# An encoder layer on one core: copies of a branch's tokens six tiles ahead, that branch's outputs kept in DRAM as 2 KB rows, and some low parts on VectorE alone

## The chip, the core and the metric

The kernel runs on one core of a Trainium2 chip. The metric is device time in microseconds (us) of one execution; three executions of the kernel before took 1133.49, 1138.85 and 1132.47, median 1133.49. A profiled execution took 1135.29 us, of which its trace covers a span of 1133.5.

The core's engines run side by side and each takes its own instructions strictly in order. In the profile PE is TensorE's matmuls and PEld its weight loads, DVE is VectorE, ACT is ScalarE, POOL is GpSimd and SP is SyncE, which here issues every DMA.

## The reference

One encoder layer is applied with the same weights to two token batches, a prompt of 512 tokens and a sample of 1024, both 1024 wide, all in fp32:

```python
h = rmsnorm(x, norm_g)
qa, ka, va, za, qb, kb, vb, zb, ga, gb = split(h @ w_in)      # 1024 -> 5376
oa = neighbourhood_attention(norm(qa), norm(ka), va, rpb_a) * silu(za)   # branch A: 8 heads of 64, 2-D window
ob = window_gqa_attention(norm(qb), norm(kb), vb, t5, sink) * silu(zb)   # branch B: 8 query heads, 2 key heads, band of 128
merged = sigmoid(ga) * (oa @ w_o_a) + sigmoid(gb) * (ob @ w_o_b)
y = x + merged @ w_out
```

## The kernel before

**Split operands.** fp32 accuracy on TensorE comes from splitting each operand into a high part (rounded by ScalarE to the matmul's type) and a low part (what is left, a subtraction), and adding three products: high by high, high by low and low by high. So `whi`/`wlo` are the parts of a weight tile, `hh`/`hl` those of the normalized tokens h, `T` holds both parts of sums of h, `pp` those of attention weights. The high part is always a ScalarE copy. The low part is a subtraction in `split` (line 1177), which may go to VectorE or to GpSimd, whichever the planner finds free first.

**Stages.** The prompt is normalized and goes through its attention; then its dense phase runs (gates z, merge gates g, the two output projections, `w_out`), during which the sample's h is made; then the sample's attention and its dense phase. The token axis is cut into tiles of 128: 4 for the prompt, 8 for the sample.

**Attention.** Six groups run one after the other, four pairs of heads of branch A (A0 to A3) and two of branch B (B0, B1). Within a group, `project` (line 764) multiplies one token tile by 384 columns of weights in 24 matmuls of 384 columns. ScalarE squares the result (`sq`, 783), VectorE sums (`ss`, 788), GpSimd turns the sum into a reciprocal root (`rs_v` 795, `rs_r` 802), VectorE scales (`qk`, 819) and TensorE transposes q and k (`x<-ident,qk`, 864). `attend` then makes scores, exponentials and outputs; the output goes from the accumulator to a tile `ot_` (1073) and from there by SP to DRAM. Since TensorE works on the projection of later tiles meanwhile, the chain from `sq` to `qk` runs beside it. Filler matmuls (`d<-hh,fh`, parts of the merge gates) are put into the gaps.

Branch B takes its tokens in another order: token tile t is every nb-th column of h (nb tiles). Those columns are first copied together into four tiles `hb` of 512 columns (two halves of `hh`, two of `hl`; lines 665 on ScalarE, 667 on VectorE). There are four `hb` buffers, one token tile's worth. The copies wait only for all of h and for a free buffer, and their priority is that of the tile before the one they serve.

**Branch outputs.** `o_d` in DRAM holds, for each channel chunk c (c below 4 is branch A, 4 to 7 branch B), 128 channels by all tokens. Branch B's outputs exist as two halves e whose sum is the output. They are stored tile by tile, in two DMAs per tile, in B's token order (line 1102). The z step of the dense phase loads them (line 1535): a block of 512 tokens in natural order is `512/nb` tokens of each of the nb tiles, so a load of the sample's half takes 8 runs of 64 values (256 B) for each channel, one of the prompt's 4 runs of 128 values (512 B). The two loaded halves are added (`ot<-ot`), multiplied with silu(z) and stored as `u_d`.

**Sums.** Most of the sample's dense phase runs a scheme with seven instead of eight products per block of four, which needs sums of h and of weights. The sums of h were stored in `t_d` during the prompt's dense phase; `stored_sums` (1245) loads them in 16 pieces of 512 columns (four sums j, four chunks k each) and splits each into parts `T`. `pair_strassen` makes weight sums `S` from raw tiles (1166) and `weight_tiles` splits them. The products `x<-T`, `d<-T` and `p<-T` (lines 1293 to 1295) need all parts.

**What sets the order.** Every operation is recorded with a priority, a duration for each engine that may take it and what it depends on. `Flow.run` then walks through a model of time and gives each engine, whenever the model says that it is free, its ready operation of best priority; the order in which it hands them out is the order of the instructions. Where VectorE and GpSimd could both take an operation, the operation carries the mark `port`; while one with that mark runs on one of the two engines in the model, no marked one is begun on the other. An operation that only VectorE may take has no such mark unless it is given one. The real order of waiting is the one on the chip; the model's times do not appear there.

Of the kernel before, what the change touches and what calls it, by code (L numbers as in the profile page):

```python
# [10 lines left out]
F32 = mybir.dt.float32  # L11
# [15 lines left out]
SLACK = 1.1  # L27
SCRATCH = 1024
# [12 lines left out]
P = 128  # L41
# [313 lines left out]
def encoder_kernel(  # L355
# [23 lines left out]
    nc = tc.nc  # L379
# [24 lines left out]
    o_d = {geo.nt: dpool.tile([2, 8, P, geo.nt], F32, tag=f"o_d{geo.nt}", name=f"o_d{geo.nt}") for geo in (gp, gs)}  # L404
# [246 lines left out]
    def attention_phase(geo, hh, hl, h_ops, mask_d, early, late):  # L651
# [79 lines left out]
        def project(br, w, t, prio):  # L731
# [10 lines left out]
            else:  # L742
# [6 lines left out]
                for q in range(2):  # L749
                    for m, v in enumerate((hh, hl)):  # L750
# [5 lines left out]
                            prio - 1, new=[hb[m][q]], hold=[v], after=[o for u in h_ops.values() for o in u], port=True,  # L756
# [204 lines left out]
        def weigh(br, gi, g, block, sums, pss, sbs, nb_t, info, prio):  # L961
# [114 lines left out]
            if br == "A":  # L1076
# [10 lines left out]
                def emit():  # L1087
                    if len(runs) == 1:
                        dst = over(o_d[nt][0, g], runs).rearrange("(i p) n -> p i n", i=2)
                        nc.sync.dma_start(dst, ot.t[:64, ::2])  # L1090
                        return
                    for i in range(2):
                        dst = over(o_d[nt][0, g, 64 * i : 64 * i + 64], runs)
# [3 lines left out]
            else:  # L1097
                for e in range(2):
                    dst = o_d[nt][e, 4 + 2 * g : 6 + 2 * g, :, runs[0][0] : runs[0][0] + P]
                    dst = dst.rearrange("c (i d) n -> d (c i) n", d=64)  # L1100
                    o = sp(
                        lambda e=e, dst=dst: nc.sync.dma_start(dst, ot.t[e * 64 : e * 64 + 64]),
                        131072, prio, use=[ot],
                    )
                    for c in (4 + 2 * g, 5 + 2 * g):
                        for n in range(nt // 512):
                            stores[c, n].append(o)
# [31 lines left out]
    def dense_phase(geo, hh, hl, h_ops, o_stores, exps_done, start, opened, tp, up, p0, p1, p2, x_t, y_t, classic, fill, after_gates=None, side=None):  # L1139
# [28 lines left out]
        def split(hi, lo, src, n, prio, new_hi, new_lo, src_v, after=()):  # L1168
# [7 lines left out]
                any_tt(n),  # L1176
# [59 lines left out]
        def stored_sums(prio, d, after):  # L1236

            tv, ops = {}, {}
            for j in (1, 2, 0, 3):
                tv[j] = tuple(f.value(tp, [P, 4, nh], F32R, "T", 8) for _ in range(2))  # L1240
                vh, vl = tv[j]
                for k in range(4):
# [7 lines left out]
                        (vh, k == 0), (vl, k == 0), [st],  # L1250
# [9 lines left out]
        def weight_tiles(operands, per, prio):  # L1260
# [5 lines left out]
            for i, src in enumerate(operands):  # L1266
                at, q = [], 0
                while q < 4:
# [7 lines left out]
                        (hi, ti not in seen), (lo, ti not in seen), [src],  # L1276
# [72 lines left out]
        def pair_strassen(srcs, post, prio, mov_h, mov_t, seed=None, last=False, kept=None):  # L1349
# [11 lines left out]
            w = weight_tiles([*first, s2, s3, s1, raw[1, 1], s4], 6, prio - 0.5)  # L1361
# [162 lines left out]
        def post_z(c, a, n, v, in_psum, prio):  # L1524
# [3 lines left out]
            for e, ot in enumerate(ots):  # L1528
                if c < 4:
                    src, dst = o_d[nt][e, c, :, a : a + n], lambda ot=ot: ot.t[:, :n]  # L1530
# [423 lines left out]
```

## Time and profile before

| | before |
|---|---|
| executions, us | 1133.49, 1138.85, 1132.47 (median 1133.49) |
| profiled execution | 1135.29 us, span of its trace 1133.5 us |
| PE | 1119.0 us busy, 6079 instructions |
| PEld | 973.2 us |
| DVE | 860.1 us, 1988 instructions |
| ACT | 651.9 us, 1499 |
| POOL | 337.3 us, 438 |
| DMA | 184.91 MB in 139010 packets on SP's queue; 167 GB/s of HBM traffic over the span |

The stages can be told apart by their matmuls: the last product of the prompt's attention (line 1066) starts 216 us from the start of the trace, its dense phase goes on to about 394, the sample's attention runs from there to about 786, and the sample's dense phase to the end. A row of the timeline gives the start of an instruction, how long it took, its engine, the line, the operation, what it writes and reads, and in brackets how long the engine had been idle before it and what ended that. An `xN` row is N like instructions in a row. The matmuls of a row overlap: one of 512 columns is shown with 0.39 us, and the next begins 0.23 us after it.

### The profile page before, as it was taken

How to read it: one execution, taken by the hardware profiler on the slowest of the kernel's cores; microseconds unless marked ns; L12 is line 12 of the kernel's file. 1: busy time of each engine (PE TensorE's matmuls, PEld its weight loads, DVE VectorE, ACT ScalarE, POOL GpSimd, SP SyncE). 2: the span in 40 equal slices, each digit the busy share in tenths (PEclk: the TensorE clock that was granted, in tenths of full speed). 3: DMA queues.
4: the chain of work that ended last, by engine and by line, in shares of the span. 5: the costliest groups of instructions: out<-in, count | busy, mean ns of one | idle time of the engine just before them, and what ended most of it. 6: DMA issues, size and time to landing. Idle time of an engine off the chain costs nothing.

```text
span 1133.5 us, 18690 instructions
## 1 busy us (share of the span) xinstructions
PE 1119.0 (99%) x6079; PEld 973.2 (86%) x6079; DVE 860.1 (76%) x1988; ACT 651.9 (58%) x1499; POOL 337.3 (30%) x438
## 2 busy tenths in 40 slices
PE   8999999999999999999999999999999999999998
PEld 6999988888888889999999988988788888888887
DVE  5888797587776568787878888885988766677764
ACT  6777987644432257565769888876543335423430
POOL 4653433000011154434324344420333322222211
PEclk9999999999999999999999999999999999999999
DMA  7854543488886732121212314244977645867862
GB/s 263 276 155 138 184 115 103 110 257 248 256 278 216 254 128 91 27 63 30 82 41 85 81 38 112 57 131 121 307 241 234 224 156 170 281 207 222 280 215 93
DMA packets 139108, 186.11 MB, mean 164 GB/s; under 512 B 29897, under 2 KB 68561, under 8 KB 139010
## 3 DMA queue, kind: packets, MB, share of 16 engines
q1 hardware_dynamic: 139010, 184.91, 51.8%
q8 instruction: 48, 0.79, 0.3%
q14 instruction: 50, 0.41, 0.1%
HBM read 137.66 MB, written 51.92 MB: 167 GB/s over the span
## 4 chain that ended last, share of the span: by engine, by line
PE 93%; DMA 2%; DVE 2%; issue 1%; ACT 1%; POOL 1%; SPq 0%; DVEq 0%; ACTq 0%
PE p L764 25%; PE x L1294 9%; PE x L1295 9%; PE x L1293 9%; PE x L1066 5%; PE x L937 5%; PE x L1029 5%; PE d L1293 4%; PE d L1295 4%; PE d L1294 4%; PE p L1294 4%; PE p L1295 4%; PE p L1293 4%; PE x L864 2%; DMA w<-in_w_att_dram 1%
## 5 line engine op out<-in xcount | busy, mean ns | idle before, releaser
L764 PE MATMUL p<-whi,hh 128*128 128x384 f32 x384 | 133.4, 348 | 0.0
L764 PE MATMUL p<-whi,hl 128*128 128x384 f32 x384 | 132.2, 344 | 0.0
L764 PE MATMUL p<-wlo,hh 128*128 128x384 f32 x384 | 131.8, 343 | 0.0
L1172 ACT ACTIVATE whi<-raw 128x512 fp32r<-128x512 f32 (+1 forms) x140 | 81.4, 600 | 71.2 <-PE x L1294 22.3
L981 ACT ACTIVATE sb<-sb,mx 128x384 f32<-128x384 f32 (+1 forms) x192 | 107.8, 565 | 16.9 <-DVE mx L972 16.5
L1295 PE MATMUL x<-T,wlo 128*128 128x512 f32 x280 | 108.9, 389 | 0.0
L1294 PE MATMUL x<-T,whi 128*128 128x512 f32 x280 | 108.9, 389 | 0.0
L1293 PE MATMUL x<-T,whi 128*128 128x512 f32 x280 | 108.9, 389 | 0.0
L764 PE MATMUL p<-whi,hb 128*128 128x384 f32 x384 | 107.6, 346 | 0.0
L1177 POOL TENSOR_TENSOR wlo<-raw,whi 128x512 fp32r<-128x512 f32 (+1 forms) x33 | 39.5, 1204 | 215.6 <-DMA raw<-in_w_g_dram 112.9
L1040 DVE TENSOR_TENSOR pp<-x,pp 128x512 fp32r<-128x512 f32 (+1 forms) x136 | 82.5, 638 | 19.6 <-ACT pp L1035 19.0
L1177 DVE TENSOR_TENSOR wlo<-raw,whi 128x512 fp32r<-128x512 f32 (+1 forms) x107 | 72.0, 682 | 32.3 <-ACT whi L1172 28.7
L802 POOL TENSOR_TENSOR rs_r<-rs_v,mhalf 128x4 f32<-128x4 f32 (+1 forms) x72 | 80.5, 1118 | 5.7
L1035 ACT ACTIVATE pp<-x 128x512 fp32r<-128x512 f32 (+1 forms) x136 | 70.8, 559 | 15.8 <-PE x L1029 14.3
L1294 PE MATMUL x<-hl,whi 128*128 128x512 f32 x200 | 77.8, 389 | 0.0
L1295 PE MATMUL x<-hh,wlo 128*128 128x512 f32 x200 | 77.8, 389 | 0.0
L1293 PE MATMUL x<-hh,whi 128*128 128x512 f32 x200 | 77.8, 389 | 0.0
L1066 PE MATMUL x<-pp,v 128*128 128x256 f32 (+1 forms) x368 | 75.8, 322 | 0.0
L764 PEld LDWEIGHTS p<-whi,hl 128*128 128x128 f32 x384 | 72.6, 189 | 1.3 <-issue 1.0
L764 PEld LDWEIGHTS p<-wlo,hh 128*128 128x128 f32 x384 | 72.7, 189 | 1.0 <-issue 0.7
L764 PEld LDWEIGHTS p<-whi,hh 128*128 128x128 f32 x384 | 72.7, 189 | 0.7 <-DVE v L812 0.3
L764 PEld LDWEIGHTS p<-whi,hb 128*128 128x128 f32 x384 | 69.1, 188 | 3.1 <-issue 1.3
(388 smaller groups left out, 2965.1 us busy)
## 6 DMA issues: line engine op xcount, KB each, us to landing
raw<-in_w_g_dram SPq DMA_DIRECT2D x84, 256.0 KB
w<-in_w_att_dram SPq DMA_DIRECT2D x46, 384.0 KB
raw<-in_w_z_dram SPq DMA_DIRECT2D x40, 256.0 KB
ot<-o_d SPq DMA_DIRECT2D x36, 256.0 KB
g_d<-C SPq DMA_DIRECT2D x34, 256.0 KB
fr<-in_w_g_dram SPq DMA_DIRECT2D x28, 256.0 KB
raw<-in_w_out_dram SPq DMA_DIRECT2D x28, 256.0 KB
out_dram<-C SPq DMA_DIRECT2D x19, 256.0 KB
```

What stands on the lines that cost most here:

```text
L764: pe.matmul(ps.t[:, :GW], part[u](k), mv.t[:, c], start=k == 0 and m == 0, stop=k == KC - 1 and m == 2,)
L802: lambda e: nc.gpsimd.tensor_tensor(r.t[:, :nn], rv.t[:, :nn], mhalf[:, :nn], op=ALU.pow),
L937: pe.matmul(pss[2 * pair + i].t[:, :width], q.t[rows, u, at : at + P], kv[:, tiles[0] : tiles[-1] + 1 : step], start=n == 0, stop=n == 2,)
L981: act.activation(sb.t[:, :width], sb.t[:, :width], AF.Exp, bias=mx.t[:, i : i + 1], scale=-1.0, accum_out=sm.t[:, i : i + 1],)
L1035: lambda e, pt=pt, pp=pp, nn=nn: act.activation(pp.t[:, 0, :nn], pt.t[:, :nn], AF.Copy),
L1040: lambda e, pt=pt, pp=pp, nn=nn: dve.tensor_tensor(pp.t[:, 1, :nn], pt.t[:, :nn], pp.t[:, 0, :nn].bitcast(F32), op=ALU.subtract),
L1066: pe.matmul(out(), v.t[:, vs], mv(), start=first, stop=last)
L1172: (("act", ACT_(n)),), lambda e: act.activation(hi(), src(), AF.Copy), prio,
L1177: lambda e: engines[e].tensor_tensor(lo(), src(), hi().bitcast(F32), op=ALU.subtract), prio,
L1293: pe.matmul(out, hi.t[:, cs], mh(), start=first and k == 0, stop=False, **more)
L1294: pe.matmul(out, hi.t[:, cs], ml(), start=False, stop=False, **more)
L1295: pe.matmul(out, lo.t[:, cs], mh(), start=False, stop=last and k == len(ws) - 1, **more)
```

## The change

1. **Copies of branch B's tokens.** The `hb` copies of a tile now also wait for the first matmul of the projection that stands six tiles (`AHEAD`) ahead of the tile before it, so those of a stage's first B tile are no longer ready as soon as h is. For later tiles the buffers decide as before.
2. **Branch B's outputs in DRAM.** They get a tensor of their own, `ob_d`, whose innermost 512 values are the 512 tokens of one block: 8 (or 4) runs of 64 (128) values, in B's order within the block. A tile of the sample is therefore stored in four DMAs of 64 by 4 by 64 values (runs of 256 B) instead of two of 64 by 4 by 128; the prompt still has two per tile. A load is now 128 rows of 512 values, 2 KB each. What the loaded block means to the multiplication is unchanged.
3. **Low parts of h's sums on VectorE.** The low parts of `T` from `t_d`, and the low parts of the weights of the first z pair of the sample (priority 0), may only go to VectorE. With one engine to choose from they lose the mark `port`.

```diff
+AHEAD = 6
@@ encoder_kernel
-    o_d = {geo.nt: dpool.tile([2, 8, P, geo.nt], F32, ...) for geo in (gp, gs)}
+    o_d = {geo.nt: dpool.tile([4, P, geo.nt], F32, ...) for geo in (gp, gs)}
+    ob_d = {geo.nt: dpool.tile([geo.nt // 512, 2, 8, 64, 512], F32, ...) for geo in (gp, gs)}
@@ project
-                            prio - 1, new=[hb[m][q]], hold=[v], after=[o for u in h_ops.values() for o in u], port=True,
+                            prio - 1, new=[hb[m][q]], hold=[v], port=True,
+                            after=[*(o for u in h_ops.values() for o in u), f.begun[nt, prio - AHEAD]],
@@ weigh, branch B
-                for e in range(2):
-                    dst = o_d[nt][e, 4 + 2 * g : 6 + 2 * g, :, runs[0][0] : runs[0][0] + P]
-                    dst = dst.rearrange("c (i d) n -> d (c i) n", d=64)
-                    o = sp(
-                        lambda e=e, dst=dst: nc.sync.dma_start(dst, ot.t[e * 64 : e * 64 + 64]),
-                        131072, prio, use=[ot],
-                    )
+                m, t = 512 // nb, runs[0][0] // P
+                for n in range(nt // 512):
+                    for e in range(2):
+                        dst = ob_d[nt][n, e, 4 * g : 4 * g + 4, :, t * m : t * m + m].rearrange("a p m -> p a m")
+                        o = sp(
+                            lambda n=n, e=e, dst=dst: nc.sync.dma_start(dst, ot.t[e * 64 : e * 64 + 64, :, n * m : n * m + m]),
+                            1024 * m, prio, use=[ot],
+                        )
@@ split
-        def split(hi, lo, src, n, prio, new_hi, new_lo, src_v, after=()):
+        def split(hi, lo, src, n, prio, new_hi, new_lo, src_v, after=(), both=True):
             ...
             b = f.op(
-                any_tt(n),
+                any_tt(n)[: 1 + both],
@@ stored_sums
-                        (vh, k == 0), (vl, k == 0), [st],
+                        (vh, k == 0), (vl, k == 0), [st], both=d is m_d,
@@ pair_strassen
-            w = weight_tiles([*first, s2, s3, s1, raw[1, 1], s4], 6, prio - 0.5)
+            w = weight_tiles([*first, s2, s3, s1, raw[1, 1], s4], 6, prio - 0.5, prio > 0)
@@ post_z
-                    src = o_d[nt][e, c].rearrange("p (i n) -> p i n", n=P)[:, :, a // nb : a // nb + m]
-                    dst = lambda ot=ot: ot.t[:, :n].rearrange("p (i n) -> p i n", n=m)
+                    src = ob_d[nt][a // nh, e].rearrange("(c i) p n -> c (i p) n", i=2)[c - 4, :, :n]
```

The number of instructions of each kind stays the same, except that the sample's branch B is stored in 64 DMAs instead of 32. Line numbers from here on are two or three higher in the changed kernel (667 for the ScalarE copies, 1180 for the low parts).

Since the planner hands out the work, the order changes beyond the edited lines. Three places follow, the last two of one stretch.

**Start of the sample's attention, VectorE.** `wlo` are the low parts of the first projection's weights; `ss`, `v` and `qk` belong to the first two token tiles. Before:

```order
L610 TENSOR_TENSOR wlo<-w_4898,whi 128x768
L788 TENSOR_REDUCE ss<-sq 128x4
L812 TENSOR_TENSOR v<-p,v 128x2x64
L667 CAST hb<-hl 128x512 x2
L788 TENSOR_REDUCE ss<-sq 128x4
L819 TENSOR_TENSOR qk<-p,rs_r 128x256
L812 TENSOR_TENSOR v<-p,v 128x2x64
```

Now:

```order
L612 TENSOR_TENSOR wlo<-w_4900,whi 128x768
L791 TENSOR_REDUCE ss<-sq 128x4
L815 TENSOR_TENSOR v<-p,v 128x2x64
L791 TENSOR_REDUCE ss<-sq 128x4
L822 TENSOR_TENSOR qk<-p,rs_r 128x256
L815 TENSOR_TENSOR v<-p,v 128x2x64
```

The two casts are gone from here, and so are the two `hb<-hh` copies that ScalarE had between its `sq` of the first two tiles. Nothing else moved on these two engines, on GpSimd or on TensorE from here until the third tile of group A3, where the four copies now stand among the work of that group. In the prompt the same four copies, which stood near the start of its attention, now stand in the third tile of group A2, and the planner put other work of the prompt's attention in another order as well.

**Sums of h in the first z pair, GpSimd.** From its last operation of the sample's attention (`sm`) to its first multiplication with an `ot`. Before:

```order
L1002 TENSOR_TENSOR sm_10358<-sm_10358,es_10380 128x4
L1177 TENSOR_TENSOR T_10748<-fh_10653,T_10738 128x512
L1177 TENSOR_TENSOR wlo_10754<-S_10678,whi_10721 128x512
L1177 TENSOR_TENSOR wlo_10805<-raw_10607,whi_10767 128x512
L1166 TENSOR_TENSOR C_10803<-C_10803,ot_10790 128x512
```

Now:

```order
L1005 TENSOR_TENSOR sm_10388<-sm_10388,es_10410 128x4
L1169 TENSOR_TENSOR S_10645<-raw_10524,S_10575 128x512
L1180 TENSOR_TENSOR wlo_10756<-S_10738,whi_10746 128x512
L1180 TENSOR_TENSOR wlo_10769<-S_10741,whi_10754 128x256
L1180 TENSOR_TENSOR wlo_10756<-S_10741,whi_10746 128x256
L1180 TENSOR_TENSOR wlo_10769<-S_10727,whi_10754 128x512
L1169 TENSOR_TENSOR S_10806<-raw_10668,S_10738 128x512
L1180 TENSOR_TENSOR wlo_10820<-raw_10654,whi_10809 128x512
L1180 TENSOR_TENSOR wlo_10820<-S_10806,whi_10809 128x256
L1169 TENSOR_TENSOR C_10723<-C_10723,ot_10725 128x512
```

GpSimd gave up one low part of T and took weight sums and weights' low parts of the second z pair: eight operations where there were three.

**The same stretch, VectorE.** `T_10748` before and `T_10785` now are the low parts of the same sum, as are `T_10815` and `T_10828`; `ot` is the sum of two loaded halves. Before:

```order
L1177 TENSOR_TENSOR T_10748<-U_10648,T_10738 128x512
L1177 TENSOR_TENSOR wlo_10754<-S_10696,whi_10721 128x256
L1166 TENSOR_TENSOR U_10760<-fr_10365,x_10643 128x512
L1177 TENSOR_TENSOR T_10748<-U_10661,T_10738 128x512
L1166 TENSOR_TENSOR ot_10676<-ot_10676,ot_10683 128x512
L1177 TENSOR_TENSOR T_10748<-w32_10666,T_10738 128x512
L1166 TENSOR_TENSOR C_10694<-C_10694,ot_10676 128x512
L1166 TENSOR_TENSOR U_10787<-U_10760,x_10740 128x512
L1166 TENSOR_TENSOR C_10803<-U_10787,d_10770 128x512
L1177 TENSOR_TENSOR T_10815<-U_10718,T_10797 128x512
```

Now:

```order
L1180 TENSOR_TENSOR T_10785<-U_10690,T_10777 128x512
L1169 TENSOR_TENSOR U_10794<-fr_10395,x_10675 128x512
L1180 TENSOR_TENSOR T_10785<-fh_10694,T_10777 128x512
L1180 TENSOR_TENSOR T_10785<-U_10700,T_10777 128x512
L1180 TENSOR_TENSOR T_10785<-w32_10707,T_10777 128x512
L1169 TENSOR_TENSOR U_10823<-U_10794,x_10771 128x512
L1180 TENSOR_TENSOR T_10828<-U_10712,T_10814 128x512
L1169 TENSOR_TENSOR ot_10725<-ot_10725,ot_10732 128x512
L1169 TENSOR_TENSOR U_10841<-U_10794,d_10802 128x512
L1169 TENSOR_TENSOR C_10848<-U_10823,d_10802 128x512
```

The sum of the two loaded halves now stands behind all four low parts of the third sum instead of between the last two, and the fourth sum's first part stands ahead of it.

On TensorE, the products of the third sum's last part (`d<-T`, which need its low part: `T_10748` before, `T_10785` now) changed places with the group `p<-T` that stood ahead of them and needs parts made earlier. Before:

```order
L1293 MATMUL p_10783<-T_10597,whi_10716 128x512
L1294 MATMUL p_10783<-T_10613,whi_10716 128x512
L1295 MATMUL p_10783<-T_10597,wlo_10729 128x512
L1293 MATMUL d_10770<-T_10738,whi_10568 128x512
L1294 MATMUL d_10770<-T_10748,whi_10568 128x512
L1295 MATMUL d_10770<-T_10738,wlo_10593 128x512
```

Now:

```order
L1296 MATMUL d_10802<-T_10777,whi_10595 128x512
L1297 MATMUL d_10802<-T_10785,whi_10595 128x512
L1298 MATMUL d_10802<-T_10777,wlo_10609 128x512
L1296 MATMUL p_10830<-T_10631,whi_10746 128x512
L1297 MATMUL p_10830<-T_10652,whi_10746 128x512
L1298 MATMUL p_10830<-T_10631,wlo_10756 128x512
```

They now begin one group of three matmuls earlier. A few groups of `p<-T` behind them, which need the fourth sum, exchanged places with `x<-T` in the same way.

More of the change, by code (lines that the diff above doesn't have):

```diff
@@ L403, in encoder_kernel @@
     t_d = dpool.tile([4, 4, P, NT_S // 2], F32, tag="t_d", name="t_d")
-    o_d = {geo.nt: dpool.tile([2, 8, P, geo.nt], F32, tag=f"o_d{geo.nt}", name=f"o_d{geo.nt}") for geo in (gp, gs)}
+    o_d = {geo.nt: dpool.tile([4, P, geo.nt], F32, tag=f"o_d{geo.nt}", name=f"o_d{geo.nt}") for geo in (gp, gs)}
+    ob_d = {geo.nt: dpool.tile([geo.nt // 512, 2, 8, 64, 512], F32, tag=f"ob_d{geo.nt}", name=f"ob_d{geo.nt}") for geo in (gp, gs)}
     s_d = dpool.tile([4, 4, P, 512], F32, tag="s_d", name="s_d")
@@ L1088, in emit @@
                     if len(runs) == 1:
-                        dst = over(o_d[nt][0, g], runs).rearrange("(i p) n -> p i n", i=2)
+                        dst = over(o_d[nt][g], runs).rearrange("(i p) n -> p i n", i=2)
                         nc.sync.dma_start(dst, ot.t[:64, ::2])
@@ L1092, in emit @@
                     for i in range(2):
-                        dst = over(o_d[nt][0, g, 64 * i : 64 * i + 64], runs)
+                        dst = over(o_d[nt][g, 64 * i : 64 * i + 64], runs)
                         nc.sync.dma_start(dst, ot.t[:64, 2 * i].rearrange("p (a b) -> p a b", b=64))
@@ L1097, in weigh @@
             else:
[L1098 to L1106 removed]
+                m, t = 512 // nb, runs[0][0] // P
[6 more added lines that the diff above has]
+                        )
+                        for c in (4 + 2 * g, 5 + 2 * g):
                             stores[c, n].append(o)
@@ L1258, in load_raw, with weight_tiles @@
             return v
-        def weight_tiles(operands, per, prio):
+        def weight_tiles(operands, per, prio, both=True):
             n = -(-len(operands) * 4 // per)
@@ L1275, in weight_tiles @@
                         lambda src=src, sc=sc: src.t[:, sc], m * P, prio,
-                        (hi, ti not in seen), (lo, ti not in seen), [src],
+                        (hi, ti not in seen), (lo, ti not in seen), [src], both=both,
                     )
@@ L1529, in post_z @@
                 if c < 4:
-                    src, dst = o_d[nt][e, c, :, a : a + n], lambda ot=ot: ot.t[:, :n]
+                    src = o_d[nt][c, :, a : a + n]
                 else:
-                    src = o_d[nt][e, c].rearrange("p (i n) -> p i n", n=P)[:, :, a // nb : a // nb + m]
-                    dst = lambda ot=ot: ot.t[:, :n].rearrange("p (i n) -> p i n", n=m)
+                    src = ob_d[nt][a // nh, e].rearrange("(c i) p n -> c (i p) n", i=2)[c - 4, :, :n]
                 dma(
-                    lambda dst=dst, src=src: nc.sync.dma_start(dst(), src), 512 * n, prio - 0.5, new=[ot],
+                    lambda ot=ot, src=src: nc.sync.dma_start(ot.t[:, :n], src), 512 * n, prio - 0.5, new=[ot],
                     after=o_stores[c, a // nh],
```

## Prediction

> **What bounds the kernel now.** I read the busy shares first, then the groups of waits of TensorE, then busy time by stretches.
>
> ```profile
> PE 1119.0 (99%) x6079; PEld 973.2 (86%) x6079; DVE 860.1 (76%) x1988; ACT 651.9 (58%) x1499; POOL 337.3 (30%) x438
> ```
> ```profile
> PE x L1811 <- DMA rb<-in_norm_row_dram: 4.4, 1, 4.4
> PE x L864 <- DVE qk L819: 3.1, 3, 1.8
> PE d L1294 <- DVE T L1177: 1.6, 1, 1.6
> ```
> ```profile
> core 0: us, PE busy (x) PEld busy (x) DVE busy (x) ACT busy (x) POOL busy (x), PEclk, DMA share, GB/s
> 30.00:402.00 372.00, 372.00 (x2005) 323.02 (x2005) 276.37 (x676) 221.25 (x496) 91.44 (x135) 1.00 0.64 200
> 402.00:470.00 68.00, 65.40 (x432) 61.40 (x430) 53.51 (x159) 40.15 (x108) 36.94 (x54) 1.00 0.26 80
> 470.00:805.00 335.00, 334.77 (x2103) 301.99 (x2102) 272.48 (x758) 248.81 (x627) 107.16 (x156) 1.00 0.29 83
> 805.00:823.00 18.00, 15.52 (x65) 11.57 (x64) 17.36 (x23) 8.04 (x16) 9.03 (x6) 1.00 0.85 274
> 823.00:1130.00 307.00, 307.00 (x1367) 254.65 (x1366) 221.62 (x330) 114.87 (x218) 79.28 (x66) 1.00 0.65 212
> ```
>
> TensorE (PE) is busy 99% of the span, at a granted clock of 1.00 in every stretch from 30 us to 1130. The change leaves the number and the shapes of the matmuls as they are, so it can only win or lose PE's idle time. Where that idle time lies, the third view says. From 30 to 402 us, the whole of the prompt, and from 823 to 1130, most of the sample's dense phase, there is none: 372.00 of 372.00 and 307.00 of 307.00. What remains is 68.00 − 65.40 = 2.60 us at the start of the sample's attention, 335.00 − 334.77 = 0.23 in the rest of it, and 18.00 − 15.52 = 2.48 at 805 to 823, the first z pair of the sample. Together 5.3 us. The first row of waits, 4.4 us for a load at the very start of the program, is out of the change's reach. So 5.3 us is the ceiling of a gain, 0.47% of the time. A loss has no such ceiling.
>
> VectorE (DVE) is next: 81% busy in the sample's attention (272.48 of 335.00) and 96% in the first z pair (17.36 of 18.00). There every added microsecond on DVE is likely to be felt by PE.
>
> **The copies, where they leave.** The start of the sample's attention in the timeline:
>
> ```profile
> 406.45 0.44 PE L864 MATMUL x<-ident,qk 128*128 128x128 f32 x2 [1.84 <-DVE qk L819]
> ...
> 402.62 2.15 DVE L667 CAST hb<-hl 128x512 fp32r<-128x512 f32 x2
> 405.97 0.42 DVE L819 TENSOR_TENSOR qk<-p,rs_r 128x256 f32<-128x256 f32 x1 [0.75 <-POOL rs_r L802]
> ...
> 402.23 1.31 POOL L1177 TENSOR_TENSOR fl<-fr,fh 128x512 fp32r<-128x512 f32 x1 [11.40 <-ACT fh L1172]
> 403.62 1.22 POOL L795 TENSOR_SCALAR rs_v<-ss 128x4 f32<-128x4 f32 x1
> 404.92 1.01 POOL L802 TENSOR_TENSOR rs_r<-rs_v,mhalf 128x4 f32<-128x4 f32 x1
> 406.02 0.19 POOL L795 TENSOR_SCALAR rs_v<-ss 128x4 f32<-128x4 f32 x1
> ```
>
> PE waits 1.84 us for `qk`, which waits 0.75 for GpSimd's `rs_r`, which follows `rs_v`. Two `rs_v` of the same size stand here: 1.22 us from 403.62, while DVE makes its two casts (402.62 to 404.77), and 0.19 us from 406.02, when none is under way. The casts are what the change takes away from this place, so I cost `rs_v` at 0.19 again: 1.22 − 0.19 = 1.03 earlier for `rs_r`, `qk` and PE. The rest of the wait stays, since `rs_v` cannot begin before `fl` ends at 403.54 and `rs_r` takes its own 1.01. **Term: −1.0.** Bounds: 0, if the casts are not what stretched `rs_v`, to −1.8, if the missing ScalarE copies bring `ss` forward too and GpSimd takes `rs_v` ahead of `fl` in effect. The order of those two is the same as before, which puts me at the middle.
>
> **The copies, where they arrive.** In the sample they go into group A3, in the prompt into A2. The casts have as long to do as before; the cover is the other tiles' projections, on which PE works while `qk` is made, and PE idles 0.23 us in all of 470 to 805 and not at all in the prompt. If the cover is gone, I price it by the stall beside which these same four copies stood: 1.84. The buffers are read by the first B tile, more than four token tiles behind, so the copies are not late. **Term: 0**, bounds −0.2 (the idle time there is) to +1.8.
>
> **The stores.** The last store of branch B stands ahead of the loads of the stored sums in SP's queue:
>
> ```profile
> 785.75 1.24 SPq L1102 DMA_DIRECT2D o_d<-ot__10494  x2
> ...
> 796.04 0.68 DVE L1177 TENSOR_TENSOR T<-fh,T 128x512 fp32r<-128x512 f32 x1
> ...
> 797.88 0.39 PE L1293 MATMUL x<-T,whi 128*128 128x512 f32 x1
> ```
>
> Four issues for two cost SP another 1.24 us per tile, at the most. For the seven tiles before, SP's queue has gaps in which this lies. For the last tile it pushes back the loads behind it; the low part that is ready at 796.72 is read from 797.88 on, so 1.16 of the 1.24 us is covered. **Term: 0**, bounds 0 to +1.2. A rule of the Trainium skill speaks against this edit: "DMA: Bandwidth & Descriptors", Specifications, wants 512 B or more in a transfer for full rate and has smaller ones done by reading, changing and writing back. The stores go from runs of 512 B to 256 B, the sample's loads from 256 B to 2 KB. By that rule the stores alone would now be slow. With the DMA engines busy 0.29 of the time in the attention, this trace leaves room for that, and the sum stays the same by the rule.
>
> **The sums of the first z pair.** This is where the order moved, and where DVE has no slack:
>
> ```profile
> 813.08 0.50 PE L1294 MATMUL d<-T,whi 128*128 128x512 f32 x1 [1.57 <-DVE T L1177]
> 818.37 0.50 PE L1294 MATMUL p<-T,whi 128*128 128x512 f32 x1 [0.24 <-DVE T L1177]
> 820.67 0.50 PE L1294 MATMUL p<-T,whi 128*128 128x512 f32 x1 [0.65 <-DVE T L1177]
> ```
> ```profile
> 806.44 0.42 DVE L1177 TENSOR_TENSOR wlo<-S,whi 128x256 fp32r<-128x256 f32 x1
> 806.77 0.68 DVE L1177 TENSOR_TENSOR T<-U,T 128x512 fp32r<-128x512 f32 x1
> 807.37 0.42 DVE L1177 TENSOR_TENSOR wlo<-S,whi 128x256 fp32r<-128x256 f32 x1
> ...
> 808.37 1.27 DVE L1177 TENSOR_TENSOR T<-U,T 128x512 fp32r<-128x512 f32 x1
> 810.10 1.25 DVE L1166 TENSOR_TENSOR ot<-ot 128x512 f32<-128x512 f32 x1 [0.46 <-DMA ot<-o_d]
> 811.27 1.75 DVE L1177 TENSOR_TENSOR T<-w,T 128x512 fp32r<-128x512 f32 x1
> ```
> ```profile
> 807.79 1.30 POOL L1177 TENSOR_TENSOR T<-fh,T 128x512 fp32r<-128x512 f32 x1 [31.89 <-DVE wlo L1177]
> 809.05 1.75 POOL L1177 TENSOR_TENSOR wlo<-S,whi 128x512 fp32r<-128x512 f32 x1
> 810.76 1.71 POOL L1177 TENSOR_TENSOR wlo<-raw,whi 128x512 fp32r<-128x512 f32 x1
> ```
> ```profile
> 801.40 0.63 ACT L1172 ACTIVATE T<-U 128x512 fp32r<-128x512 f32 x1 [3.15 <-DMA U<-t_d]
> ```
> ```profile
> 793.90 3.66 SPq L1520 DMA_DIRECT2D u_d<-C  x1
> ```
>
> PE waits 1.57 us for the third sum's last low part, which ends on DVE at 811.27 + 1.75 = 813.02, and 0.24 + 0.65 = 0.89 for the fourth sum. Work on DVE that now stands behind that last part: the wait for `ot` (0.46) and `ot` (1.17 to the next start), two low parts of weights of 256 columns (0.33 each, as from 806.44 to 806.77) and one of 512 that stands ahead of these (0.68 as for `T<-fh` at 796.04); together 3.0. The second sum's first low part moves into the time ahead, 0.6 less; the `fh` part that GpSimd made from 807.79 comes to DVE, 0.6 more. Own work: −3.0.
>
> Against it stands what GpSimd does meanwhile. A low part of 512 columns takes DVE 0.68 alone and up to 1.75 beside a GpSimd operation (811.27): a hold of 1.07. Before, GpSimd had three operations in this stretch; now it has eight, some 12 us of work at 1.3 to 1.75 us each, and the low parts have lost the mark that kept the planner from setting the two side by side. If all four low parts of the third sum are held, this is 4 × 1.07 = 4.28, of which 0.59 (808.37) and 1.07 (811.27) were there already: +2.6. Both together: −0.4. PE asks for that part a group earlier, and a group of three matmuls takes 813.08 to 813.65 in like rows, some 0.7 us, so the stall there ends near 1.57 − 0.4 + 0.7 = 1.9: +0.3. The 0.89 us behind it I take as gone. The fourth sum's first part stands ahead of `ot`, and its loads come earlier: SP was held 3.66 us on one `u_d` store behind the two loads of `ot` in 256 B runs, and ScalarE stood 3.15 us for a stored sum behind it. With 128 rows in place of 1024 runs for each `ot` load, I expect about 3 us of that back. **Term: +0.3 − 0.9 = −0.6.** Bounds: −2.5, all of the idle time, if GpSimd's operations fall elsewhere; and +3.7, if five low parts are held (5 × 1.07 = 5.35, less the 1.66 that was there) and the work taken off DVE only filled time in which it would have waited.
>
> **Sum.** −1.0 + 0 + 0 − 0.6 = −1.6. The span of 1133.5 becomes 1131.9 and the profiled execution's own 1135.29 becomes 1133.7. That execution lay 1.8 above the median of the runs, 1133.49, so the median becomes **1131.9 us**.
>
> **Rivals.**
>
> *All stalls of the sums go.* The DVE's own work that leaves (3.0) is more than the stall (1.57). It needs GpSimd to be out of the way in the 5 us before the third sum's last part; eight operations in the place of three speak against it. −1.0 − 2.5 = −3.5: 1130.0.
>
> *GpSimd holds the low parts back.* One mechanism, on DVE between the second sum and the fourth: operations that the planner kept apart now stand side by side, and every low part pays 1.07. It decides as soon as all four low parts of the third sum are held and the loads of `ot` were not what delayed the sums: the 3.0 us that I took off then come back onto the forecast's stall, and the term goes from −0.6 to +2.4 and, with a fifth part held, to its bound of +3.7. With the −1.0 of the start this is +2.7: 1136.2. For it: 811.27, 1.75 beside 810.76, 1.71. Against it: GpSimd's new operations need weights that come by DMA, so they may start late. The Trainium skill has the rule: "SBUF — State Buffer", Who interferes with whom, has a VectorE operation with two inputs in SBUF and a GpSimd operation share one port that is locked whole, so that one blocks until the other is done. The rows above agree with it.
>
> *Nothing moves.* If `rs_v` was slow for another reason than the casts, and the third sum waits as before, 1133.5.
>
> **How the numbers follow.** Forecast 0.55 (its own range 1129.5 to 1133.5), all stalls go 0.20, GpSimd holds 0.15, nothing moves 0.10. The forecast's time is the likeliest. 0.5% of the time, about what a measurement of this kernel can tell from no change, is 5.7 us: faster means below 1127.8, slower above 1139.2. All the idle time in reach is 5.3 us, so faster is left with 0.08, mostly from runs that scatter. Slower needs +3.7, +1.8 and +1.2 at once, or a loss in a place that had no stall: 0.08. Same 0.84. The range reaches down past the second case to 1128.0 and up past the third to 1137.0.
>
> **What would show it.** In the changed kernel's profile: `rs_v` near 403.6 takes about 0.2 us, and PE's wait for `qk` falls from 1.84 to about 0.8. The `u_d` store at about 794 is issued in well under 1 us, and ScalarE's wait for a stored sum at about 801 is gone. The third sum's low parts on DVE take about 1.7 us each, with GpSimd busy beside them, and PE waits about 1.9 us once. Stretches 30 to 402 and 823 to 1130 stay without idle time. Wrong would be: idle time of PE in group A3 or in the prompt, where copies or other work now stand; PE waiting over 4 us in the sums; or a total that moves while PE's idle time does not.

## The result and the profile after

The changed kernel is slower: 1141.42 us, median of 8 executions (1138.74 to 1143.22), against 1134.47 of the kernel before (8 executions). The ratio is 1.0057, 95% interval 1.0039 to 1.0075: clear of 1, while the 0.5% that the prediction set as its bound for slower lies inside the interval. The forecast was 1131.9, the range 1128 to 1137. The profiled execution took 1141.28 us, its span is 1139.5, 6.0 longer than before.

The same views as before, of the changed kernel: busy shares, waits of TensorE (us in total, times, longest), busy time by stretches (the columns as in the prediction).

```profile
PE 1122.3 (98%) x6079; PEld 973.7 (85%) x6079; DVE 854.2 (75%) x1963; ACT 650.0 (57%) x1500; POOL 360.7 (32%) x462
```
```profile
PE d L1297 <- DVE T L1180: 2.3, 4, 0.7
PE x L867 <- DVE qk L822: 2.1, 3, 0.8
PE p L1297 <- DVE T L1180: 1.1, 2, 0.7
...
PE p L1296 <- ACT whi L1175: 0.8, 1, 0.8
PE d L1296 <- ACT fc L1618: 0.6, 2, 0.4
PE p L767 <- DVE v L815: 0.5, 1, 0.5
PE x L1296 <- ACT fl L1650: 0.4, 1, 0.4
PE x L1297 <- DVE hl L1180: 0.2, 1, 0.2
```
```profile
30.00:220.00 190.00, 189.22 (x1187) 170.55 (x1188) 149.07 (x434) 146.50 (x371) 92.92 (x139) 1.00 0.51 155
220.00:350.00 130.00, 130.00 (x575) 107.69 (x574) 93.09 (x185) 58.91 (x103) 6.49 (x5) 1.00 0.80 241
350.00:402.00 52.00, 50.99 (x228) 41.80 (x227) 29.53 (x44) 13.25 (x20) 6.05 (x4) 1.00 0.74 245
...
755.00:805.00 50.00, 49.04 (x248) 39.45 (x247) 31.88 (x73) 33.00 (x76) 3.63 (x8) 1.00 0.56 159
805.00:830.00 25.00, 21.53 (x89) 15.89 (x89) 23.94 (x30) 12.42 (x25) 14.96 (x11) 1.00 0.67 237
830.00:1130.00 300.00, 300.00 (x1325) 248.43 (x1324) 215.22 (x317) 112.52 (x214) 80.58 (x68) 1.00 0.66 218
```

The wait for `qk` fell from 3.1 to 2.1 us and its longest from 1.8 to 0.8. But the list is longer: waits that were not there before stand in the prompt's attention (`p` for `v`, 0.5), in its dense phase (`hl` 0.2, `whi` 0.8), near the end of the sample's attention (`fc`, `fl`), and the waits for parts of sums grew from 1.6 + 0.9 to 2.3 + 1.1. TensorE now idles 0.78 us before 220 and 1.01 between 350 and 402, stretches without a microsecond of idle time before. From 830 on there is none, as before.

A wait that the list shows is not all that TensorE loses around it, so the account of the whole 6.0 us goes by the starts of the matmuls. All kernels have 6079 of them. Where the copies moved, their order differs (from 34 to 217 us and from 565 to 646), and so it does in a few places of the first z pair; elsewhere the n-th matmul does the like work in each, and at the seven marks of the table the same work lies behind. The table gives, for seven such matmuls, by how much its start moved against the kernel before in each step (worked out from the traces; the first column from the start of the program to 30 us, the others from the mark on its left, in times of the kernel before):

| kernel | to 30 | 30–223 | 223–400 | 400–472 | 472–755 | 755–794 | 794–827 | sum |
|---|---|---|---|---|---|---|---|---|
| changed | +0.4 | +0.7 | +2.1 | −1.1 | +0.5 | +1.4 | +2.0 | +6.0 |
| copies alone | +1.0 | +1.1 | +2.1 | +0.6 | +0.5 | +0.1 | −1.1 | +4.2 |
| rows alone | −1.1 | +1.1 | 0.0 | +1.0 | 0.0 | 0.0 | −3.6 | −2.6 |
| VectorE low parts alone | +0.6 | +3.9 | +0.3 | +3.8 | 0.0 | 0.0 | +2.0 | +10.6 |
| copies and rows | +1.4 | +1.4 | +0.2 | −1.2 | +0.5 | +1.5 | −3.6 | +0.2 |
| changed, marked | −0.4 | +1.6 | +2.1 | +0.7 | +0.5 | +1.6 | −1.2 | +4.9 |
| rows and marked low parts | −1.2 | +0.8 | 0.0 | −0.8 | 0.0 | 0.0 | −1.2 | −2.4 |
| rows, copies in the sample | +0.5 | +0.2 | 0.0 | −0.8 | +0.5 | +0.7 | −3.6 | −2.6 |
| rows, copies in the prompt | −0.1 | +0.9 | +1.2 | −1.0 | +0.1 | +1.0 | −3.7 | −1.5 |
| rows and the sums' low parts | −0.9 | 0.0 | +4.1 | +2.0 | 0.0 | 0.0 | +1.6 | +6.8 |
| four stores, old rows | −0.2 | +1.4 | +0.2 | −0.2 | 0.0 | 0.0 | −0.6 | +0.7 |
| rows, copies in the prompt, 3 ahead | +0.2 | +4.0 | +0.3 | +0.1 | 0.0 | 0.0 | −3.7 | +1.0 |

Each row is one execution. How much of a number is scatter, the rows with like order tell: VectorE low parts alone and rows alone have the order of the kernel before up to about 790 us, and still the first shows +3.9 and +3.8 in the second and fourth column; its profiled execution, at 1145.91 us, was the slowest of its own. So the first, second and fourth columns scatter by microseconds, the third once (+4.1, in the kernel whose profiled execution was again the slowest of its runs, 1142.03 us). The next two show 0.0 in every kernel that keeps the old order there but one: rows with the copies later in the prompt has the old order on all engines from 323 us on, and still +0.1 and +1.0 (more on this at the stores, below). In the last, like orders agree to 0.1 us: −3.6 or −3.7 five times, −1.2 twice. What the whole program takes is told by the timed runs, below.

### The profile page after: what moved, and what is told of

Its sections match the earlier page's. It is cut to its first block, busy times and chain, and to the rows that moved or that the text cites. A ratio compares the mean times of both kernels' runs of the same rounds, so it can differ in the third digit from the quotient of the medians.

```text
span 1139.5 us, 18735 instructions
## 1 busy us (share of the span) xinstructions
PE 1122.3 (98%) x6079; PEld 973.7 (85%) x6079; DVE 854.2 (75%) x1963; ACT 650.0 (57%) x1500; POOL 360.7 (32%) x462
## 4 chain that ended last, share of the span: by engine, by line
PE 85%; DMA 6%; DVE 4%; issue 2%; ACT 1%; POOL 1%; SPq 1%; DVEq 0%; ACTq 0%; POOLq 0%
PE p L767 25%; PE x L1297 8%; PE x L1296 7%; PE x L1298 7%; PE x L1069 5%; PE x L1032 5%; PE x L940 5%; PE d L1296 4%; PE d L1298 4%; PE d L1297 4%; PE p L1297 4%; PE p L1296 4%; PE p L1298 4%; PE x L867 2%; DMA raw<-in_w_out_dram 1%
## 5 line engine op out<-in xcount | busy, mean ns | idle before, releaser
L1180 DVE TENSOR_TENSOR wlo<-raw,whi 128x512 fp32r<-128x512 f32 (+1 forms) x106 | 74.3, 710 | 36.9 <-ACT whi L1175 35.7
L805 POOL TENSOR_TENSOR rs_r<-rs_v,mhalf 128x4 f32<-128x4 f32 (+1 forms) x72 | 83.1, 1154 | 5.5
```

What stands on the lines that cost most here:

```text
L805: lambda e: nc.gpsimd.tensor_tensor(r.t[:, :nn], rv.t[:, :nn], mhalf[:, :nn], op=ALU.pow),
L1180: lambda e: engines[e].tensor_tensor(lo(), src(), hi().bitcast(F32), op=ALU.subtract), prio,
```

## The experiments

All times are medians; the kernel before, timed beside them, had 1135.14, 1134.7 and 1135.23 us in the three sessions, each on a chip of its own (the first four kernels, the next four, the last three). So kernels of different sessions are compared by their ratios to it. A place such as 145, 356 or 385 us keeps its name though it stands a few us earlier or later in each trace.

### One edit at a time, and two

*Copies alone.* Only the `AHEAD` wait of the copies.

> The copies of branch B's tokens later, and nothing else. Theory 1, each edit pays in its own place: TensorE's wait for qk at 404 us falls from 1.84 us to about 0.8, and the prompt's attention, whose order moves with this edit alone, loses about 0.7 us (in the changed kernel 0.68 us ahead of the first product of B's tokens at 145 us); together -0.4, about 1134 us. Theory 2, the loss of 6 to 7 us comes from late loads in the dense phases, which any reordering of the prompt can cause: this kernel too is 2 us or more slower, with TensorE waiting at about 356 and 385 us.

Measured: 1139.3 us, ratio 1.0032 (1.0015 to 1.0048). Neither theory's number in full, but nearer the second: over 2 us slower, and TensorE waits 1.2 us for `whi` at 385 us (386.9 in this trace), the same place as in the changed kernel, while at 356 there is nothing.

*Rows alone.* `ob_d`, its stores in four pieces and its loads.

> Branch B's outputs as 2 KB rows, stored in four pieces, and nothing else. Theory 1: the prompt's dense phase loses the 2.1 us that the changed kernel lost at 356 and 385 us, because the transfers around it stand otherwise; the u_d store at 794 us is issued in under 1 us in place of 3.66, and of the 2.5 us of waits in the first z pair about 1 goes; together +1, about 1135.5. Theory 2: the rows are not the cause, TensorE does not wait at 356 and 385, and the kernel is 1 us faster, 1133.5 or less.

Measured: 1131.79 us, ratio 0.9963 (0.9948 to 0.9978). This is a gain, and larger than either theory gave. TensorE waits for no part of a sum at all in the first z pair:

```profile
786.00:830.00 44.00, 44.00 (x196) 36.36 (x194) 36.74 (x59) 25.51 (x49) 12.26 (x7) 1.00 0.83 280
```

SP's queue differs. First the kernel before, then rows alone (start, duration of the issue, what is written and read):

```profile
791.71 2.14 SPq L1535 DMA_DIRECT2D ot<-o_d  x2
793.90 3.66 SPq L1520 DMA_DIRECT2D u_d<-C  x1
```
```profile
794.91 1.72 SPq L1535 DMA_DIRECT2D ot<-ob_d  x2
796.90 0.32 SPq L1521 DMA_DIRECT2D u_d<-C  x1
```

Behind two loads of 1024 runs each, the next issue is held 3.66 us, and with it every load queued after it. Behind two loads of 128 rows it takes 0.32.

*Low parts on VectorE alone.* `both` in `split`, for the sums and for the first z pair's weights.

> Low parts of the sums and of the first z pair's weights on VectorE alone, and nothing else; the order moves only from 790 us on. Theory 1, GpSimd's other operations hold them: the waits in the first z pair grow from 2.5 us by 2 to 3, low parts of 512 columns take 1.2 to 1.8 us with GpSimd busy beside them, and the kernel comes to about 1137. Rival: those stalls do not depend on who makes the parts but on the loads; then within 0.5 us of before, 1134.5.

Measured: 1139.4 us, ratio 1.0032 (1.0015 to 1.0048). The way of the first theory, not its sizes: TensorE's waits for parts of sums are 3.6 us against 2.5, 1.1 more where 2 to 3 were expected, and the kernel is slower than the 1137 expected.

```profile
PE d L1294 <- DVE T L1177: 1.9, 4, 0.7
PE p L1294 <- DVE T L1177: 1.7, 2, 1.0
```

*Copies and rows.*

> Copies later and rows of 2 KB, with low parts on either engine as before. Theory 1: the sum of these two edits alone, about +0.6, 1135. If the losses outside the first z pair (prompt's attention 0.7, 356 and 385 us 2.1, 761 us 0.7, against -1.2 at 404) are those of these two edits, +2.5 or a little more, 1137; the loss of the low parts then is the rest of the 6.5.

Measured: 1135.52 us, ratio 1.0005 (0.9991 to 1.002). As the sum of the two alone (+0.32% − 0.37% = −0.05%), within the intervals. So the copies cost 0.42% on top of the rows, 3.7 us by the medians and 4.8 by the ratios, and the low parts the rest, 1.0057 − 1.0005 = 0.52% or 5.9 us, more on top of the rows than alone (0.32%): they take back what the rows had won in the first z pair (column 794–827: −3.6 with copies and rows, +2.0 in the changed kernel).

### The low parts: the mark, or the work

*The changed kernel, marked.* One word in `split`, so that a low part that only VectorE may take is again kept apart from GpSimd's operations in the planner's model:

```diff
-                use=src_v, after=[a, *after], **{**kw(*new_lo), ...},
+                use=src_v, after=[a, *after], port=True, **{**kw(*new_lo), ...},
```

> The changed kernel, but the low parts that only VectorE may take carry the mark again that keeps the planner from setting a GpSimd operation beside them. Theory 1, the lost mark is the price of this edit: low parts of 512 columns take 0.7 us again, TensorE's waits in the first z pair fall from 3.4 us to under 0.5, and the kernel comes to about 1136, where it was with copies and rows alone (1135.5). Rival, VectorE simply has too much work there: little changes, 1140 to 1141.5.

Measured: 1139.62 us, ratio 1.0029 (1.0013 to 1.0045). Between the two theories: 0.28% of the 0.52% are won back. The intervals of the two kernels overlap; the last column of the table, where like orders agree to 0.1 us, says the same: −1.2 with the mark, +2.0 without, −3.6 with the low parts on either engine.

*Rows and marked low parts*, the copies as before:

> Rows of 2 KB and low parts on VectorE with the mark, copies as before. Theory 1: as the rows alone, 1131.8, within 1 us. If VectorE without GpSimd's help is too slow in the first z pair: 2 us or more above the rows alone.

Measured: 1134.18 us, ratio 0.9989 (0.9976 to 1.0001), 2.4 us above the rows alone by the medians, 0.26% by the ratios. So in both kernels the mark is about half of the price. In both kernels the wait for `d<-T` is gone and one for `p<-T` is left, 1.8 us in two pieces. VectorE and GpSimd there, in rows and marked low parts:

```profile
811.69 1.78 DVE L1178 TENSOR_TENSOR T<-U,T 128x512 fp32r<-128x512 f32 x1
813.39 1.08 DVE L1167 TENSOR_TENSOR C<-C,ot 128x512 f32<-128x512 f32 x1
814.39 1.78 DVE L1178 TENSOR_TENSOR T<-fh,T 128x512 fp32r<-128x512 f32 x1
```
```profile
811.17 1.75 POOL L1167 TENSOR_TENSOR S<-raw,S 128x512 f32<-128x512 f32 x1
813.97 1.65 POOL L1167 TENSOR_TENSOR S<-raw 128x512 f32<-128x512 f32 x1 [1.06 <-issue]
```

Operations that the planner had kept apart in its model meet on the chip all the same; its times are not the chip's. What put these beside each other was not followed. With the rows alone, the first of the fourth sum's low parts is GpSimd's:

```profile
811.88 1.29 POOL L1178 TENSOR_TENSOR T<-U,T 128x512 fp32r<-128x512 f32 x1
```

*Rows and the sums' low parts*, with the weights' low parts on either engine and no mark. Edit on top of rows and low parts: `weight_tiles(..., prio - 0.5)` without `prio > 0`.

> Rows of 2 KB, and of the low parts only those of the sums of h bound to VectorE, without the mark; weights' low parts on either engine. Theory: the sums' low parts are the whole of that edit's price, since GpSimd's order in the first z pair is nearly that of rows with the whole edit: TensorE waits 3 us there, and the kernel comes 5 us above the rows alone, 1136.5 to 1137. Rival, the weights' low parts matter: 1132 to 1134.

Measured: 1137.38 us, ratio 1.0026 (1.0015 to 1.0037); 0.63% above the rows alone, the theory. TensorE waits 2.2 + 1.1 us for parts of sums. The binding of the weights' low parts is not needed for the loss.

### The copies: prompt or sample

*Rows, copies later in the sample only*, and *in the prompt only*:

```diff
-    after=[*(o for u in h_ops.values() for o in u), f.begun[nt, prio - AHEAD]],
+    after=[*(o for u in h_ops.values() for o in u), f.begun[nt, prio - AHEAD] if nt == NT_S else None],
```

(`NT_P` for the other.)

> Rows of 2 KB, and the copies later in the sample only; the prompt's order is that of before. Theory: the price of the copies lies mostly in the prompt's attention (0.7 at 145 us and about 0.5 more before 220). In the sample they gain 1 us at 404 and lose about 0.6 in small steps between 560 and 760, 0.7 at 761 and 0.6 at 796: together +0.9 on the rows alone, 1132.7. Rival, the price lies in the sample: 1135.

> Rows of 2 KB, and the copies later in the prompt only. Theory: the prompt's part of the price, 1.5 to 2.5 us on the rows alone: 1133.3 to 1134.3. Rival, the price lies in the sample: 1132.

Measured: sample only 1132.47 us, ratio 0.9978 (0.9966 to 0.9991); prompt only 1134.68, ratio 0.9996 (0.9984 to 1.0008). On the rows alone the sample's copies cost 0.15%, which the intervals do not tell from nothing, and the prompt's 0.33%, 3.7 us. The price is mainly that of the prompt's copies, as the theory had it, but it is more than the 1.5 to 2.5 us expected. Not all of it is paid in the prompt: in the trace of this kernel 1.0 us comes at 761 us, in the sample's attention, where the order is that of the rows alone.

*Rows, copies in the prompt, three tiles ahead*: `AHEAD = 3`.

> Rows of 2 KB and the copies later in the prompt only, but three tiles ahead in place of six. Theory, the price of the prompt's copies (3 us on the rows alone) is that of their standing among the busy tiles on VectorE and ScalarE: closer to their use it is as much or more, 1134.5 to 1136. Rival, it is that of the one order that the planner happened to come to: then another order, another price, between 1131.5 and 1137, and TensorE's waits at 145, 356 and 385 us change place.

Measured: 1135.38 us, ratio 1.0003 (0.9991 to 1.0014); the price of six tiles again, within the intervals. The waits did change place. At 145, 356 and 385 us there is nothing above 0.2, and at 124.6 and 128.4 us of its trace stand new ones, the second because a copy is late:

```profile
PE p L767 <- DVE hb L669: 1.3, 1, 1.3
```

So the time agrees with the first theory and the places with the rival. That it must be so for every number of tiles is not shown.

### The stores

*Four stores, old rows.* The kernel before, with the sample's stores split into four and the old place in DRAM:

```diff
-    o = sp(lambda e=e, dst=dst: nc.sync.dma_start(dst, ot.t[e * 64 : e * 64 + 64]), 131072, ...)
+    m = P * 512 // nt
+    for n in range(nt // 512):
+        o = sp(lambda ...: nc.sync.dma_start(dst[:, :, n * m : n * m + m], ot.t[e * 64 : e * 64 + 64, :, n * m : n * m + m]), 1024 * m, ...)
```

> The kernel before, with branch B's outputs in their old place in DRAM but stored in four pieces a tile (runs of 64 values in place of 128) in the sample. The order on TensorE, VectorE, ScalarE and GpSimd is that of the rows alone, so this tells the order and the number of stores from the rows of the loads. Theory, the 2 KB loads are the gain: the u_d stores are again issued in over 3 us, stored sums come late, TensorE waits 2 us or more in the first z pair, and the kernel stands at 1134 to 1136. Rival, the order is the gain: 1132.

Measured: 1136.09 us, ratio 1.0017 (1.0005 to 1.0029). On TensorE, VectorE, ScalarE and GpSimd the order is that of the rows alone, and by the two ratios the time is 0.54% longer. The stores are in runs of 256 B in both, so the gain is that of the loads in 2 KB rows. SP's queue in this kernel:

```profile
795.14 2.03 SPq L1538 DMA_DIRECT2D ot<-o_d  x2
797.23 3.23 SPq L1523 DMA_DIRECT2D u_d<-C  x1
```

The `u_d` store is held again, 3.23 us, and TensorE waits 1.8 us for parts of sums.

## Why the prediction was wrong

**The ceiling.** The places where a gain could lie were read rightly, their size was not. The prediction gave the sums 2.48 us, and the rows alone win 3.6 there. A wait costs TensorE more than the idle time that its row shows. The longest one, in the kernel before:

```profile
811.11 0.40 PE L1293 MATMUL d<-T,whi 128*128 128x512 f32 x1
813.08 0.50 PE L1294 MATMUL d<-T,whi 128*128 128x512 f32 x1 [1.57 <-DVE T L1177]
813.41 0.40 PE L1295 MATMUL d<-T,wlo 128*128 128x512 f32 x1
```

The starts are 1.97 and 0.33 us apart, where such matmuls start every 0.23 us: 1.84 us are lost, 0.27 more than the 1.57 shown, since the 0.40 us of the matmul ahead, which the profile counts as busy, cover part of the wait. At 809.15 in the same trace 0.28 us are lost with no wait shown at all. By the starts the sums had some 3.5 us to win, about what the rows won.

**The other side** was not worked out. The prediction noted that a loss has no ceiling, and then priced every stretch in which TensorE did not idle at nothing. Of the 6.0 us of the pair of traces, +0.7, +2.1, +0.5 and +1.4, together 4.7, came in stretches where TensorE had idled 0.2 us before. (The +0.7 alone would prove nothing, since that column shows 0.0 to +3.9 in kernels that keep the old order there.)

**The copies, where they leave: −1.0, measured −1.1 in this pair, the size by luck.** `rs_v` was stretched by the casts, as the prediction had it. Without them, changed kernel:

```profile
405.82 0.19 POOL L798 TENSOR_SCALAR rs_v<-ss 128x4 f32<-128x4 f32 x1
406.10 1.02 POOL L805 TENSOR_TENSOR rs_r<-rs_v,mhalf 128x4 f32<-128x4 f32 x1
```

The two take 0.19 and 1.02 us in all five kernels whose sample's copies are moved. In the eight whose casts stay, either `rs_v` takes 1.2 and `rs_r` 1.0 (five kernels), or `rs_v` takes about 0.5 and `rs_r` 1.3 (three). In the changed kernel the first transposes no longer wait at all: by the starts 2.0 us are gone, twice the term. Half of that is `rs_v`; the other half is that ScalarE has the weights (`whi`, 402.57, before 400.34) only 2.2 us later than before, while TensorE comes 3.2 us later. And a second wait, 0.9 us by the starts, stands behind the first, that of the next tile's transposes, whose `qk` is queued on VectorE behind biases that wait for the load of the mask. Its rows, changed kernel:

```profile
408.58 1.50 DVE L700 TENSOR_TENSOR bias<-mask,raw 128x192 f32<-128x192 f32 x5 [0.81 <-DMA mask<-in_mask_s_dram]
410.00 0.41 DVE L822 TENSOR_TENSOR qk<-p,rs_r 128x256 f32<-128x256 f32 x1
```
```profile
410.47 0.44 PE L867 MATMUL x<-ident,qk 128*128 128x128 f32 x2 [0.83 <-DVE qk L822]
```

With copies alone VectorE waited 2.34 us for that load and TensorE as long. In the changed kernel with the mark the first transposes waited 2.28 us after all, since the weights ahead of them in the queues landed late. So the column 400–472 goes from −1.2 to +0.7 among these five kernels, and from −1.0 to +3.8 among the others, and the timed runs show no gain of the sample's copies. The term was right for `rs_v`; what is late next was not asked, and the loads of this place decide it from run to run.

**The copies, where they arrive: 0, bounds −0.2 to +1.8. This step failed.** The timed price of all copies on top of the rows is 0.42%, 4 to 5 us, where the term was 0; of it the prompt has 0.33%. I costed the moved copies by themselves, as work with cover, and not the prompt's new order, which the front of this document mentions. One of its places can be followed to its cause. In the changed kernel at 145 us, VectorE and GpSimd:

```profile
140.50 0.61 DVE L669 CAST hb<-hl 128x512 fp32r<-128x512 f32 x1
141.15 1.97 DVE L1086 TENSOR_TENSOR ot__2172<-ot__2172 64x256 f32<-64x256 f32 x1
...
145.44 0.21 DVE L815 TENSOR_TENSOR v<-p,v 128x64 fp32r<-128x64 f32 x1
```
```profile
140.86 1.97 POOL L612 TENSOR_TENSOR wlo<-w,whi 128x768 fp32r<-128x768 f32 x1 [3.71 <-ACT whi L607]
```
```profile
145.79 0.41 PE L767 MATMUL p<-whi,hb 128*128 128x384 f32 x1 [0.52 <-DVE v L815]
```

An addition in `ot_` that takes VectorE 0.42 us (143.88 in the same trace has the like) takes 1.97 beside GpSimd's low part, VectorE comes to `v` late, and TensorE waits for the accumulator that `v` is read from. The wait stands at 145 us in all five kernels that move the prompt's copies six tiles ahead, and in none of the others. It is some 0.5 us, a small part of the price. Two more go with the same edit and not so regularly, by the starts of the matmuls: 356 us (0 to 0.5 us by kernel) and 385 us (0 to 1.4; 1.9 and 0.5 us at 354 and 356 also once in a kernel whose order there is the old one), where work on the sample's h and loads of `w_out`'s tiles come later. Their order is the same as before from 284 us on; what differs is the order from 230 to 284 and when loads land. Which of the two it is was not settled, so most of the price of the prompt's copies is placed by the timed runs alone, without a cause that was followed. In the sample, the five kernels that move its copies show +0.5 in the column 472–755, all others 0.0 or +0.1.

**The stores: 0, bounds 0 to +1.2.** This step failed too, though only beside the copies. In rows alone SP took 2.56 us for the last tile's four issues, and no wait of TensorE follows. In the changed kernel ScalarE, at the end of the sample's attention, waits for that store to land, and TensorE for what ScalarE makes next:

```profile
793.27 1.28 ACT L1516 ACT_TABLE_LOAD   x1 [2.85 <-DMA ob_d<-ot__10526]
```
```profile
797.02 0.50 PE L1296 MATMUL x<-hh,whi 128*128 128x512 f32 x1 [0.43 <-ACT fl L1650]
```

By the starts this is 0.7 us. It stands so in all four kernels that have both the four stores and the sample's copies moved. With the copies alone, two stores, ScalarE waits 1.91 us and TensorE not; where the sample's copies stay, ScalarE does not wait there. Why moving the copies brings ScalarE to wait for this store was not followed. The prediction followed the stores only to the loads behind them in SP's queue.

The other half of the +1.4 in the column 755–794 stands at 761 us, in the four kernels with the rows and the prompt's copies six tiles ahead, and in no other. Rows with the copies in the prompt shows it best: TensorE waits 0.79 us for ScalarE's `fc`, and that for a store queued behind the four of a tile of branch B:

```profile
759.99 0.60 ACT L1618 ACTIVATE fc<-d 128x512 f32<-128x512 f32 x1 [2.06 <-DMA p_d<-fc]
```

Neither edit alone has it (+0.1 and 0.0), so here 1.4 us of the 6.0 belong to two edits together; why this store lands late in these four is open. With 256 B runs in the stores and 2 KB in the loads the kernel is faster all the same, and with 256 B in both it is 0.17% slower than before.

**The sums of the first z pair: −0.6, bounds −2.5 to +3.7; measured +2.0.** The sum put two large terms against each other, and both were there. What the rows give back was sized too low (−3.6 alone), and what the low parts cost too low by more (from −3.6 to +2.0, 5.6 us). VectorE, GpSimd and TensorE in the changed kernel:

```profile
811.79 1.23 DVE L1180 TENSOR_TENSOR T<-U,T 128x512 fp32r<-128x512 f32 x1
...
813.73 0.99 DVE L1180 TENSOR_TENSOR T<-fh,T 128x512 fp32r<-128x512 f32 x1
814.64 1.77 DVE L1180 TENSOR_TENSOR T<-U,T 128x512 fp32r<-128x512 f32 x1
816.33 1.77 DVE L1180 TENSOR_TENSOR T<-w,T 128x512 fp32r<-128x512 f32 x1
```
```profile
808.56 5.61 POOL L1180 TENSOR_TENSOR wlo<-S,whi 128x512 fp32r<-128x512 f32 x4 [8.03 <-ACT whi L1175]
814.13 1.73 POOL L1169 TENSOR_TENSOR S<-raw,S 128x512 f32<-128x512 f32 x1
815.82 1.73 POOL L1180 TENSOR_TENSOR wlo<-raw,whi 128x512 fp32r<-128x512 f32 x1
```
```profile
814.77 0.50 PE L1297 MATMUL d<-T,whi 128*128 128x512 f32 x1 [0.73 <-DVE T L1180]
816.46 0.50 PE L1297 MATMUL d<-T,whi 128*128 128x512 f32 x1 [0.73 <-DVE T L1180]
818.16 0.50 PE L1297 MATMUL d<-T,whi 128*128 128x512 f32 x1 [0.73 <-DVE T L1180]
```

Of GpSimd's eight operations the first runs at 799.00; the other seven run without a gap from 808.56 to 818.7. All four low parts of the third sum are held, two of them to 1.77 us against 0.68 alone, two to less (1.23 and 0.99), together for 3.0 us where the forecast took 4.28. TensorE, which uses one every 0.7 us, gets one every 1.7. Its wait became 2.3 us where 1.9 was forecast, but it came in four pieces, and each piece costs some 0.27 more than it shows: by the starts the third sum lost 1.3 us against the kernel before, not 0.3. A further 0.4 was lost at an earlier sum (801.73), whose low part stands behind one of a weight that is held, 1.78 us from 799.29, beside the first of the eight.

The step that failed most in this term is the one after it, "the 0.89 us behind it I take as gone": it became 1.1. The hold passes on to the fourth sum. ScalarE makes that sum's high parts behind a `C` for which it waits 4.52 us for VectorE (821.13), and the low part at 823.48 is held again, 1.76 us. With the rows alone the 0.89 is gone, as forecast, so it is the low parts that keep it. By "SBUF — State Buffer" in the Trainium skill, section "Who interferes with whom", a VectorE operation with two inputs in SBUF contends with a GpSimd operation that reads SBUF, and the order of issue decides which of them blocks. The rows above agree: 1.77 beside 1.73, by turns.

**The chances.** The rival that GpSimd holds the low parts back had 0.15 and a time of 1136.2. Its mechanism is what happened in the sums. That the time is 5 us above it comes of losses outside the first z pair, of the copies and of the copies beside the stores, for which there was no rival at all. The bound of 1137 was the sum of known edits; a stretch of the prompt of some 250 us (34 to 284) in a new order should have carried its own unknown cost.

## What to carry to other kernels

Where the bounding engine has no idle time, a new order can only lose there: cost a replanned stretch by what its neighbours can hold up, not by the instructions that moved. Edits that come together should be timed apart; here one won 0.4% alone, the other two lost 0.3% each alone and more beside it, and the rows alone, at 0.9963 (0.9948 to 0.9978) of the kernel before, are the version to keep. Before work is bound to one engine, look at what the planner will give the freed engine to do beside it.

## What was not expected of the hardware

A DMA of many short runs can hold back the queue that issued it, well after its own issue. In the four kernels with the old rows, SP needed 2.99 to 3.78 us for the issue behind two loads of 1024 runs of 256 B (the two pairs at 791 to 813 us); with loads of 128 rows of 2 KB, the same bytes, 0.32 to 1.22. It is not always so: later pairs of such loads, at 846, 852 and 866 us of the kernel before, let the next issue through in 0.61 to 0.65. What makes the difference was not followed.

When both engines have work in line, VectorE and GpSimd do not always alternate. In rows and marked low parts one GpSimd operation of 512 columns took

```profile
806.24 3.72 POOL L1178 TENSOR_TENSOR wlo<-S,whi 128x512 fp32r<-128x512 f32 x1 [31.51 <-ACT whi L1173]
```

while VectorE went through six of its own at 0.42 to 0.69 us each: there GpSimd was the one that lost, 3.72 us against 1.29 for the next one, and VectorE felt nothing.
